# The last 512 tokens of x modulated with tokens on partitions and turned by transposing DMAs

## The chip, the cores and the metric

The kernel runs on one core of one Trainium2 chip. The metric is the device time of one execution in microseconds (us). Executions of the same kernel agree to some tenths of a per cent.

## What is computed

One decoder layer on 2048 tokens of width 1024, in float32. Cut to what matters here:

```python
mod = silu(c) @ w_ada + b_ada
shift, scale, gate = split(mod, 3)
h = rms_norm(x, g_pre) * (1.0 + scale) + shift      # modulated input
proj = h @ w_in                                     # qa ka va fa za qb kb vb zb
oa = forgetting_attention(qa, ka, va, fa + b_fgate) * silu(za)      # causal, 8 heads
ob = sliding_window_sink_attention(rope(qb), rope(kb), vb, sinks) * silu(zb)   # window 128
y = concat(oa, ob) @ w_out
x = x + gate * rms_norm(y, g_post)
```

`h` is what the change is about: each token's row is scaled by the reciprocal root of its mean square, then multiplied by a vector over the 1024 features (`g_pre * (1 + scale)`) and added to another (`shift`). The projections need `h` with the features on the partitions, in two float16 parts (high and low) whose sum carries the float32 value.

## The kernel before

Tokens are handled in four chunks of 512 (`CH`). The projection input of chunk `ci` is the tile `hT[ci]`, 128 partitions (a feature within a group of 128) by two parts by eight feature groups by 512 tokens. `hT[3]` also holds x of chunk 1 for a while, before it is filled.

How a chunk is brought there, in four helpers (chunks 1 to 3): `load_x` (L404) fetches x by SyncE, 128 tokens on the partitions. `squares` (L412) has ScalarE square and sum each tile of 128 tokens, `root` (L419) computes the reciprocal roots `rst`, three small operations on VectorE and the rest on GpSimd. `normal` (L423) multiplies each tile by its `rst` on VectorE. `turn(ci, k)` (L431) then takes feature group `k`: TensorE transposes four 128 by 128 blocks into a PSUM tile `px`; ScalarE applies the scale `Gp` and the shift `Shp` as one value for each partition, once into the float32 tile `hf` and, for even `k`, once more into the high part; VectorE makes the high part for odd `k` and subtracts it from `hf` to give the low part. `turn_x` (L450) queues the second and third step one and two ticks later. The `hf` tiles rotate among three buffers.

The order of the work is written out by hand. `punits` is a list of units of TensorE work: a kb or a z projection of a chunk is eight units of three matmuls (`proj_units`, L342), a vb projection eight units of twelve narrow ones, a turn is a unit of its own. `fill` (L1119) runs the units in order. Before unit number `n` it runs what `at_slice(n, ...)` (L1000) has put there, and every two units `tick` (L205) runs what `after(m, ...)` has deferred by `m` ticks. Every engine works through its instructions in the order in which they were issued. The weights of each projection are fetched, scaled and split by functions that `add` (L962) puts at fixed distances ahead of the first use: `w_load`, `w_max` (the maximum on VectorE and a store of 128 values `mx_d` by GpSimd), `w_back` (read back to all partitions as `mxr`), `w_scale`, `w_high`, `w_low`, `w_done`.

Three PSUM banks `bk` serve the projections in turn; a bank is taken with a group's first unit and freed by the step that empties it on VectorE: the cos step of kb (L754), the low part of vb (L807 and L809), the product of z (L392). A kb projection's rotary step swaps halves by four DMAs on SyncE's queue (`qs`, L751), needs them seven ticks later (L764), and then stores the result in `kst` by four more (L779). `spread` (L455) issues eight DMAs that fill the cosine and sine tables of a chunk.

Chunk 2 has, in this order, kb (units 64 to 71), vb, zb0 of chunk 2 and zb1 of chunks 0 and 1. Before the change the eight turns of chunk 3 stand among vb, zb0 and zb1. Then come kb and vb of chunk 3, the rest of the sliding-window attention, the forgetting attention over eight heads, and the output projection, in which the attention's result is fetched by transposing DMAs from HBM (`dma_start_transpose`, L1483).

Of the kernel before, what the change touches and what calls it, by code (L numbers as in the profile page):

```python
# [10 lines left out]
F32 = mybir.dt.float32  # L11
F16 = mybir.dt.float16
# [3 lines left out]
AF = mybir.ActivationFunctionType  # L16
ALU = mybir.AluOpType
AX = mybir.AxisListType

P = 128  # L20
S = 2048
D = 1024
KT = D // P
# [8 lines left out]
VB = P + 8  # L32
# [11 lines left out]
def hybrid_layer(  # L44
# [17 lines left out]
    V, A, G, PE, SP = nc.vector, nc.scalar, nc.gpsimd, nc.tensor, nc.sync  # L62
# [6 lines left out]
    dram = ctx.enter_context(tc.tile_pool(name="dram", bufs=1, space=DRAM))  # L69
# [7 lines left out]

    o_d = [dram.tile([CH, D], F32, name="o_d0")] + [dram.tile([4, 2, P, D], F16, name=f"o_d{t}") for t in range(1, NCH)]
    z_d = dram.tile([KT, P, S], F32, name="z_d")
    mx_d = [dram.tile([P, 1], F32, name=f"mx_d{n}") for n in range(3)]  # L80


    def sm(n, tag):
        return small.tile([P, n], F32, tag=tag, name=tag)
# [7 lines left out]
    def rsqrt_mean(dst, ss, n, eng=None):  # L92

        for _ in rsqrt_parts(dst, ss, n, eng=eng):
            pass
# [45 lines left out]
    def early_pool(name, bufs):  # L141
        return early.enter_context(tc.tile_pool(name=name, bufs=bufs, side="right", reuse_waits="tile"))

    xin, hst, vbw = early_pool("xin", 4), early_pool("hst", 3), early_pool("vbw", 1)
    trig = early_pool("trig", 1)
    swx = ExitStack()
    swc = swx.enter_context(tc.tile_pool(name="swc", bufs=1))

    hT = [(hpool if i < 2 else hlate).tile([P, 2, KT, CH], F16, name=f"hT{i}") for i in range(NCH)]
# [3 lines left out]
    Gp = const.tile([P, KT], F32, name="Gp")  # L153
    Shp = const.tile([P, KT], F32, name="Shp")
# [47 lines left out]
    def after(n, f):  # L202
        late.append([n, f])
# [198 lines left out]
    xt, rstd, xlate = {}, {}, {}  # L402
# [9 lines left out]
    def squares(ci, us=range(4)):  # L412
        if ci not in rstd:
            rstd[ci] = sm(4, "ss"), sm(4, "rst")
        for u in us:
            junk = hst.tile([P, D], BF16, tag="junk", name="junk", bufs=1)
            A.activation(junk[:], xt[ci * 4 + u], AF.Square, accum_out=rstd[ci][0][:, u:u + 1])

    def root(ci):  # L419
        ss, rst = rstd[ci]  # L420
        rsqrt_mean(rst, ss[:], 4, G if ci else None)

    def normal(ci, us=range(4)):  # L423
        for u in us:
            t, r = ci * 4 + u, rstd[ci][1][:, u:u + 1]
            if ci == 0:
                A.activation(xt[t], xt[t], AF.Copy, scale=r)
            else:
                V.tensor_scalar(xt[t], xt[t], r, None, op0=ALU.mult)

    def turn(ci, k, px=None):  # L431

        px = px or ps_x.tile([P, CH], F32, tag="x", name="px")
        for u in range(4):
            PE.transpose(px[:, u * P:(u + 1) * P], xt[ci * 4 + u][:, k * P:(k + 1) * P], ident[:])
        hf = hst.tile([P, CH], F32, tag="hf", name="hf")
        hi, lo = hT[ci][:, 0, k, :], hT[ci][:, 1, k, :]

        def scaled():
            for dst in ([hi] if k % 2 == 0 else []) + [hf[:]]:  # L440
                A.activation(dst, px[:], AF.Identity, scale=Gp[:, k:k + 1], bias=Shp[:, k:k + 1])

        def split():
            if k % 2:
                V.tensor_copy(hi, hf[:])
            V.tensor_tensor(lo, hf[:], hi, op=ALU.subtract)

        return scaled, split

    def turn_x(ci, k):  # L450
        scaled, split = turn(ci, k)
        after(1, scaled)
        after(2, split)

    def spread(g):  # L455

        gr, gc = slice(32 * g, 32 * g + 32), slice(g * CH, (g + 1) * CH)
        for r in range(4):
            rr = slice(32 * r, 32 * r + 32)
            SP.dma_start(cosT[rr, gc], cs_[gr, :])  # L460
            SP.dma_start(sinT[rr, gc], (sp_ if r % 2 else sn_)[gr, :])
# [4 lines left out]
    with tc.manual_schedule():  # L466
# [94 lines left out]
        rest, parts = TWO_PI, []  # L561
# [211 lines left out]
    def kb_units(ci):  # L773
        cols_ = slice(ci * CH, (ci + 1) * CH)

        def finish(stg):
            for g in range(2):
                for h in range(2):
                    SP.dma_start(kst[g][64 * h:64 * h + 64, :, cols_], stg[64 * g:64 * g + 64, :, :])  # L779

        return proj_units("kb", ci, evac_rope(ci, finish, stp))
# [178 lines left out]
    pkeys, punits = [], []  # L960

    def add(key, us):  # L962
        if key in ("va01", "va23"):
            for j in key[2:]:
                add(f"va{j}", [])
        elif key not in pkeys and key not in ("kb", "vb"):
            at = len(punits) - {"za3": 4}.get(key, 20 if key[:2] == "za" else 0)
            for n, (lead, f) in enumerate(((42, lambda: w_load(key, pieces(key))), (31, lambda: w_max(key)),
                                           (21, lambda: w_back(key)), (12, lambda: w_scale(key)),
                                           (9, lambda: w_high(key)), (7, lambda: w_low(key, 0)),  # L970
                                           (5, lambda: w_low(key, 1)), (4, lambda: w_done(key)))):
                if n >= 4 and key[:2] in ("qk", "za"):
                    lead -= 1
                if n < 4 and key == "qb0":
                    lead += (16, 14, 12, 4)[n]
                if key[:2] in ("zb", "va"):
                    lead += {"va0": 26, "va2": 26, "zb3": 18}.get(key, 8)
                if n == 0 and key in ("qk1", "za0"):
                    lead += 8
                if key == "zb1":  # L980
                    lead = at - (6, 38, 46, 67, 71, 73, 75, 77)[n]
                if key == "zb0":
                    if n >= 3:
                        events.setdefault((13, 13, 14, 15, 16)[n - 3], []).append(f)
                else:
                    events.setdefault(max(at - lead, n), []).append(f)
        if key not in pkeys:
            pkeys.append(key)
        punits.extend(us)
# [10 lines left out]
    def at_slice(n, f):  # L1000
        events.setdefault(n, []).append(f)
# [17 lines left out]
    for ci in range(NCH):  # L1019
        n0 = len(punits)  # L1020
        add("kb", kb_units(ci))
        add("vb", vb_units(ci))
        if ci < 3:
            add(*others[ci])
            if ci == 2:
                add(*others[4])
                add(*others[5])

            mine, punits[n0:] = punits[n0:], []
            at_ = ([14, 16, 17, 18, 19, 20, 21, 22], [6, 8, 10, 12, 14, 16, 18, 20], [14, 16, 18, 20, 22, 24, 26, 28])[ci]  # L1030
            for n, u in enumerate(mine):
                punits.append(u)
                if n in at_:
                    punits.append(lambda ci=ci, k=at_.index(n): turn_x(ci + 1, k))
            if ci < 2:

                for u in range(4):
                    at_slice(n0 + (24 if ci else 9) + u, lambda ci=ci, u=u: squares(ci + 2, (u,)))
                    at_slice(len(punits) + (4 if ci else -10) + u, lambda ci=ci, u=u: normal(ci + 2, (u,)))
                at_slice(len(punits) - (3 if ci else 18), lambda ci=ci: root(ci + 2))  # L1040
            at_slice((12, 22, 30)[ci], lambda ci=ci: spread(ci + 1))
    n0 = len(punits)
    at_slice(n0, lambda: open_fox())
# [287 lines left out]
    class Step:  # L1331
# [30 lines left out]
        def low(self):  # L1362
            V.tensor_tensor(self.ph[:, 1, :self.w], self.p32[:, :self.w], self.ph[:, 0, :self.w], op=ALU.subtract)  # L1363
# [271 lines left out]
    with tc.manual_schedule():  # L1635
# [35 lines left out]
        for s, stp_ in enumerate(steps):  # L1671
            hd, r = divmod(s, NS)
# [111 lines left out]
```

## Time and profile before

| | |
|---|---|
| median of 3 runs | 1157.41 us (1156.38 to 1158.7) |
| the profiled execution | 1157.8 us |
| its span, first to last instruction | 1156.1 us |
| TensorE busy | 1116.8 us, 97% |
| VectorE busy | 930.5 us, 80% |
| ScalarE busy | 661.4 us, 57% |
| kb of chunk 2, first matmul | 90.9 us |
| kb of chunk 3, first matmul | 123.63 us |

How to read it: a line of the timeline has the start and the length in us, the engine (PE TensorE, PEld its weight load, DVE VectorE, ACT ScalarE, POOL GpSimd, SPq the queue of SyncE), the line of the program, the operation, output and inputs by the program's names, the count, and in brackets the idle time before it with what ended it. A line of the groups has the count, the busy time in us and the mean length of one in ns. A line of the waits has who waited for whom, us in total, how often, and the longest. A line of the windows has the stretch, then for each engine the busy time and count, then the granted TensorE clock, the DMA share and GB/s.

### The profile page before, as it was taken

The numbers are of one execution on the slowest core, as the hardware profiler recorded it, in microseconds if no ns is written. First come the engines' busy times: TensorE is split into PE (matmuls) and PEld (weight loads), VectorE is DVE, ScalarE is ACT, GpSimd is POOL, SyncE is SP. The second block draws the span as 40 slices with busy tenths as digits, with TensorE's granted clock in tenths as the row PEclk, the third lists the DMA queues.
The fourth block names the chain that finished last, engine by engine and source line by source line (L and its number), as shares of the span: only waits on it lengthen the run. The fifth ranks groups of instructions, "written<-read, shape, count | busy, mean of one in ns | idle before, by whom it ended". The sixth has DMA issues, their size and how long they took to land. (4 is left out here: it accounts for less than half of the span.)

```text
span 1156.1 us, 25291 instructions
## 1 busy us (share of the span) xinstructions
PE 1116.8 (97%) x9869; PEld 656.3 (57%) x9869; DVE 930.5 (80%) x2137; ACT 661.4 (57%) x1150; POOL 207.5 (18%) x332
## 2 busy tenths in 40 slices
PE   5899999999999999999999999999999999999997
PEld 2475544577765866555555555555555555544444
DVE  7877468987888568788988899888888887878885
ACT  2876344654555421666757666666776778534332
POOL 1122134554556530010010110001000000000000
PEclk9899999999999999999999999999999999999999
DMA  9943355433243232442344342123311337686743
GB/s 333 336 116 72 87 78 96 97 63 90 52 92 88 58 87 58 73 108 29 80 64 87 84 67 70 38 49 76 45 43 34 91 101 206 140 225 197 199 135 109
DMA packets 123476, 120.10 MB, mean 104 GB/s; under 512 B 64948, under 2 KB 100828, under 8 KB 123356
## 3 DMA queue, kind: packets, MB, share of 16 engines
q1 hardware_dynamic: 112088, 85.69, 27.6%
q0 software_dynamic: 10832, 32.50, 13.5%
q8 instruction: 77, 1.26, 0.6%
q14 instruction: 43, 0.35, 0.1%
q10 hardware_dynamic: 436, 0.28, 0.1%
HBM read 64.75 MB, written 25.18 MB: 78 GB/s over the span
## 5 line engine op out<-in xcount | busy, mean ns | idle before, releaser
L1356 ACT ACTIVATE p<-sta,lift,scl_qk 128x1024 f32<-128x1024 f32 (+2 forms) x160 | 172.0, 1075 | 131.6 <-PE sta L1350 82.6
L351 PE MATMUL bk<-hT,wh_qk 128*128 128x512 f16 x768 | 194.7, 378 | 0.0
L1363 DVE TENSOR_TENSOR pha<-p,pha 128x1024 f16<-128x1024 f32 (+2 forms) x160 | 169.1, 1057 | 0.2 <-ACT pha L1360 0.2
L1303 DVE TENSOR_REDUCE a_m<-bk 128x1 f32<-128x512 f32 x192 | 130.4, 686 | 45.8 <-PE bk L1300 44.8
L1576 PE MATMUL bk<-wohl,oz 128*128 128x512 f16 x744 | 165.3, 379 | 1.1 <-DVE oz L1525 0.7
L1360 ACT ACTIVATE pha<-p 128x1024 f16<-128x1024 f32 (+2 forms) x160 | 148.1, 926 | 5.9 <-PE poa L1376 1.2
L1576 PEld LDWEIGHTS <-oz 128*128 128x128 f16 x744 | 71.9, 99 | 82.8 <-DVE oz L1525 1.8
L1376 PE MATMUL poa<-vt,pha 128*128 128x65 f16 x1088 | 116.1, 192 | 1.4 <-DVE pha L1363 1.2
L1373 PE MATMUL poa<-vt,pha 128*128 128x65 f16 x1088 | 116.6, 193 | 0.8 <-DVE ona L1382 0.7
L1375 PE MATMUL poa<-vt,pha 128*128 128x64 f16 x1088 | 116.6, 194 | 0.0
L351 PEld LDWEIGHTS <-wh_qk 128*128 128x128 f16 x768 | 72.1, 97 | 74.4 <-issue 2.1
L1349 PE MATMUL sta<-T 128*128 128x512 f16 (+1 forms) x320 | 110.9, 346 | 2.8 <-ACT p L1356 2.7
L1300 PE MATMUL bk<-T 66*128 66x512 f16 (+2 forms) x320 | 109.7, 348 | 2.4 <-DVE a_m L1303 1.9
L1373 PEld LDWEIGHTS <-pha 128*128 128x128 f16 x1088 | 101.5, 96 | 15.5 <-DVE ona L1382 1.9
L1350 PE MATMUL sta<-T 69*128 69x512 f16 (+1 forms) x320 | 109.8, 348 | 0.0
L1375 PEld LDWEIGHTS <-pha 128*128 128x128 f16 x1088 | 100.9, 97 | 11.4
L1376 PEld LDWEIGHTS <-pha 128*128 128x128 f16 x1088 | 100.8, 99 | 1.8 <-DVE pha L1363 1.7
L351 PE MATMUL bk<-hT,wh_za 128*128 128x512 f16 x384 | 99.7, 378 | 0.0
L369 PE MATMUL bk<-wh_va,hT 128*128 128x256 f16 x768 | 91.9, 273 | 0.0
L351 PE MATMUL bk<-hT,wh_zb 128*128 128x512 f16 x384 | 91.6, 379 | 0.2 <-DVE qc L754 0.2
L351 PE MATMUL bk<-hT,wh_qb 128*128 128x512 f16 x384 | 91.2, 379 | 0.0
L369 PEld LDWEIGHTS <-hT 128*128 128x128 f16 x768 | 73.3, 98 | 12.2 <-issue 2.1
(459 smaller groups left out, 1919.7 us busy)
## 6 DMA issues: line engine op xcount, KB each, us to landing
hT<-in_x_dram SPq DMA_DIRECT2D x20, 512.0 KB
wa<-in_w_ada_dram SPq DMA_DIRECT2D x16, 512.0 KB
z_d<-tz POOLq DMA_DIRECT2D x32, 256.0 KB, 3.0
T<-z_d SPq DMA_DIRECT2D x16, 512.0 KB
T<-stq SPq DMA_DIRECT2D x62, 128.0 KB
out_dram<-hT SPq DMA_DIRECT2D x15, 512.0 KB
xt<-in_x_dram SPq DMA_DIRECT2D x12, 512.0 KB
qs<-qf SPq DMA_DIRECT2D x80, 64.0 KB
```

What stands on the lines that cost most here:

```text
L351: PE.matmul(ps, whl[:, a, k, :], hT[ci][:, b, k, :], start=(k == 0 and n == 0), stop=(k == KT - 1 and n == 2))
L369: PE.matmul(ps[:, (u % 2) * 2 * P:(u % 2 + 1) * 2 * P], hT[ci][:, a, k, u * P:(u + 1) * P], wv[p][:, b, k, :], start=(k == 0 and n == 0), ...
L1303: V.tensor_reduce(m3[:, u, pc:pc + 1], mx[:, :w], axis=AX.X, op=ALU.max)
L1349: PE.matmul(self.st[:, o:o + w], T[:, 3, kb_], T[:, 1, qc], start=True, stop=False)
L1350: PE.matmul(self.st[:, o:o + w], T[0:XR, 2, kb_], T[0:XR, 0, qc], start=False, stop=not diag)
L1356: A.activation(self.p32[:, :self.w], self.st[:, :self.w], AF.Exp, scale=scl[f"qk{self.hd}"][:], bias=lift[:])
L1360: A.activation(self.ph[:, 0, :self.w], self.p32[:, :self.w], AF.Copy)
L1363: V.tensor_tensor(self.ph[:, 1, :self.w], self.p32[:, :self.w], self.ph[:, 0, :self.w], op=ALU.subtract)
L1373: PE.matmul(po[:, u, :], ph[:, 0, pq], vt[:, b, hd, 0:65], start=(self.first and n == 0 and u == 0), stop=False)
L1375: PE.matmul(po[:, u, 0:64], ph[:, 0, pq], vt[:, b, hd, 65:VW], start=False, stop=False)
L1376: PE.matmul(po[:, u, :], ph[:, 1, pq], vt[:, b, hd, 0:65], start=False, stop=(self.last and n == len(self.blocks) - 1))
L1576: PE.matmul(py, self.hl[:, i, k, :], w_slot(8 * j + k)[:, cc], start=(k == 0 and m_ == 0), stop=(k == KT - 1 and m_ == 2))
```

## The change

For chunk 3 alone the turns go. The scale and shift vectors, which lie as columns (`Gp`, `Shp`, 128 by 8), are stored to HBM as two rows of 1024 (`store_cols`) and read back to all partitions as `rowG` and as a row in the buffer of vb's raw weights (`fetch_rows`). `flat(3, u)` takes a tile of 128 tokens as it lies: two VectorE operations over 1024 features (times `rst` times the scale row, plus the shift row), a ScalarE copy to float16 one tick later (high part), a VectorE subtraction another tick later (low part), and two transposing DMAs on SyncE's queue, out of the two parts into `hT[3]`. The parts use the rotating `hf` buffers. The eight turns leave the list, so all later units come eight positions sooner, with their deferred work and the weight functions counted from them. The squares of chunk 3 move from units 56 to 59 to units 46, 48, 50 and 52, its root from 61 to 55; the normal steps at 68 to 71 are replaced by `flat` at 64, 70, 76 and 82. Chunks 0 to 2 keep their way.

```diff
+    g_d = dram.tile([2, D], F32, name="g_d")
...
-    trig = early_pool("trig", 1)
+    trig, rowp = early_pool("trig", 1), early_pool("rowp", 1)
+    rowG = rowp.tile([P, D], F32, name="rowG")
...
+    rows_ = []
+
+    def store_cols():
+        for n, col_ in enumerate((Gp, Shp)):
+            SP.dma_start(g_d[n].rearrange("(k p) -> p k", p=P), col_[:])
+
+    def fetch_rows():
+        rows_.append(vbw.tile([P, KT, VB], F32, tag="wraw", name="rowS")[:].rearrange("p k n -> p (k n)")[:, 0:D])
+        for n, row_ in enumerate((rowG[:], rows_[0])):
+            SP.dma_start(row_, g_d[n].partition_broadcast(P))
+
+    def flat(ci, u):
+
+        t, r = ci * 4 + u, rstd[ci][1][:, u:u + 1]
+        parts = [hst.tile([P, D], F16, tag="hf", name="hh") for _ in range(2)]
+        V.scalar_tensor_tensor(xt[t], xt[t], r, rowG[:], op0=ALU.mult, op1=ALU.mult)
+        V.tensor_tensor(xt[t], xt[t], rows_[0], op=ALU.add)
+
+        def low():
+            V.tensor_tensor(parts[1][:], xt[t], parts[0][:], op=ALU.subtract)
+            for b in range(2):
+                SP.dma_start_transpose(hT[ci][:, b, :, u * P:(u + 1) * P], parts[b][:])
+
+        after(1, lambda: A.activation(parts[0][:], xt[t], AF.Copy))
+        after(2, low)
...
-            at_ = ([14, 16, 17, 18, 19, 20, 21, 22], [6, 8, 10, 12, 14, 16, 18, 20], [14, 16, 18, 20, 22, 24, 26, 28])[ci]
+            at_ = ([14, 16, 17, 18, 19, 20, 21, 22], [6, 8, 10, 12, 14, 16, 18, 20], [])[ci]
...
-            if ci < 2:
-
+            if ci == 0:
                 for u in range(4):
-                    at_slice(n0 + (24 if ci else 9) + u, lambda ci=ci, u=u: squares(ci + 2, (u,)))
-                    at_slice(len(punits) + (4 if ci else -10) + u, lambda ci=ci, u=u: normal(ci + 2, (u,)))
-                at_slice(len(punits) - (3 if ci else 18), lambda ci=ci: root(ci + 2))
+                    at_slice(9 + u, lambda u=u: squares(2, (u,)))
+                    at_slice(22 + u, lambda u=u: normal(2, (u,)))
+                at_slice(14, lambda: root(2))
+            if ci == 1:
+                at_slice(20, store_cols)
+                at_slice(34, fetch_rows)
+                for u in range(4):
+                    at_slice(46 + 2 * u, lambda u=u: squares(3, (u,)))
+                    at_slice(64 + 6 * u, lambda u=u: flat(3, u))
+                at_slice(55, lambda: root(3))
```

## The prediction

> **What bounds the kernel now.** I read the page first (busy time, slices), then the stretch of the change by windows, then its timeline engine by engine, then the waits and SyncE's queue.
>
> ```profile
> span 1156.1 us, 25291 instructions
> ...
> PE 1116.8 (97%) x9869; PEld 656.3 (57%) x9869; DVE 930.5 (80%) x2137; ACT 661.4 (57%) x1150; POOL 207.5 (18%) x332
> ...
> PE   5899999999999999999999999999999999999997
> ```
>
> TensorE (PE) is busy from the second slice to the last, so whatever shifts its work near 100 us shifts the end by as much: all later work is issued by position in the list of PE units, not by time. The change acts between the kb projection of chunk 2 (units 64 on) and that of chunk 3. Units are the entries of the list `punits`; chunk 2 has 40 of them beside its eight turns.
>
> ```profile
> 90.90 4.70 PE L351 MATMUL bk<-hT,wh_kb 128*128 128x512 f16 x21
> 97.02 0.38 PE L351 MATMUL bk<-hT,wh_kb 128*128 128x512 f16 x1 [1.43 <-DVE hT L445]
> ...
> 105.04 0.81 PE L351 MATMUL bk<-hT,wh_zb 128*128 128x512 f16 x3 [0.22 <-DVE qc L754]
> ...
> 107.42 0.60 PE L435 MATMUL px<-ident,xt 128*128 128x128 f32 x4
> ...
> 109.15 0.60 PE L435 MATMUL px<-ident,xt 128*128 128x128 f32 x4
> ...
> 123.63 5.34 PE L351 MATMUL bk<-hT,wh_kb 128*128 128x512 f16 x24
> ...
> 128.81 5.84 PE L795 MATMUL bk<-wh_vb,hT 128*128 128x136 f16 x96
> ...
> 134.49 1.67 PE L351 MATMUL bk<-hT,wh_qb 128*128 128x512 f16 x7
> ```
>
> A group of 24 matmuls takes 128.81 - 123.63 = 5.18 us, a vb group 134.49 - 128.81 = 5.68. Chunk 2 is one kb, one vb and three z groups: 4 x 5.18 + 5.68 = 26.4 us of 123.63 - 90.90 = 32.7. Two z units and one turn take 109.15 - 107.42 = 1.73; two z units alone 2 x 5.18 / 8 = 1.30; so a turn costs PE 0.43, not the 4 x 0.27 of its records, and eight cost 3.5 us. The remaining 2.8 are waits, most of them the one of 1.43 for `hT` of chunk 2 and its neighbours. So PE could save 6.3 us at most.
>
> ```profile
> 90.00:123.60 33.60, 31.46 (x229) 19.18 (x228) 22.85 (x49) 19.68 (x34) 7.23 (x19) 1.00 0.34 77
> ```
>
> In the same stretch VectorE (DVE) works 22.85 of 33.6 us. It has room before, but the change adds to it and shortens the stretch.
>
> **Part by part: the sizes.** The new operations have near relatives of the same shape.
>
> ```profile
> L1363 DVE TENSOR_TENSOR pha<-p,pha 128x1024 f16<-128x1024 f32 x96 | 116.8, 1217 | 0.2 <-ACT pha L1360 0.2
> ...
> L1360 ACT ACTIVATE pha<-p 128x1024 f16<-128x1024 f32 x96 | 101.2, 1054 | 2.1
> ...
> L441 ACT ACTIVATE hf<-px,Shp,Gp 128x512 f32<-128x512 f32 x30 | 22.9, 781 | 2.8 <-DVE hT L446 2.3 <-PE px L435 0.4
> ...
> L446 DVE TENSOR_TENSOR hT<-hf,hT 128x512 f16<-128x512 f32 x32 | 22.0, 692 | 5.5 <-ACT hf L441 5.0
> ...
> L1605 DVE SCALAR_TENSOR_TENSOR hT<-hT,y_rs 128x1024 f32<-128x1024 f32 x15 | 19.2, 1277 | 0.0
> ...
> L1506 DVE TENSOR_TENSOR T<-of,T 128x1024 f32<-128x1024 f32 x12 | 14.7, 1225 | 0.5
> ...
> L445 DVE CAST hT<-hf 128x512 f16<-128x512 f32 x16 | 6.8, 426 | 0.3 <-ACT hf L441 0.2
> ...
> L429 DVE TENSOR_SCALAR xt<-xt,rst 128x1024 f32<-128x1024 f32 x8 | 5.9, 787 | 2.4 <-POOL rst L122 2.4
> ```
>
> DVE loses 4 x 0.79 (normal) + 4 x 0.43 (casts) + 8 x 0.69 (low parts) = 10.4 us and gains 4 x (1.28 + 1.23 + 1.22) = 14.9 (scale by row, add row, low part). ScalarE (ACT) loses 12 x 0.78 = 9.4 and gains 4 x 1.05 = 4.2. PE loses the 3.5. DVE then has 22.9 + 4.5 = 27.4 us of work in a stretch that PE wants to do in 26.4: DVE is the bound of the stretch, and the order of its queue decides.
>
> **When the new work can start.** `flat(0)` needs `rst` of chunk 3. Before, that waited for the squares, which ACT did among the last turns of chunk 2 (this also caused PE's wait of 1.43). They now come earlier, so this wait goes. But `root(3)` stands behind the rotary step of kb(1), L764, in DVE's queue.
>
> ```profile
> 78.53 2.44 SPq L751 DMA_DIRECT2D qs<-qf  x4
> ...
> 78.78 0.54 POOL L230 DMA_DIRECT2D mx_d<-w_mx  x1 [0.50 <-DVE w_mx L227]
> ...
> 87.32 0.69 DVE L764 TENSOR_TENSOR qs<-qs,sinT 128x512 f32<-128x512 f32 x1 [3.32 <-DMA qs<-qf]
> ...
> 95.87 0.17 DVE L101 TENSOR_SCALAR rs_v<-ss 128x4 f32<-128x4 f32 x1 [1.52 <-ACT junk L417]
> ...
> 96.34 0.22 POOL L108 TENSOR_SCALAR rs_v<-rs_v 128x4 f32<-128x4 f32 x1 [9.02 <-DVE rs_h L106]
> ...
> 100.44 0.20 POOL L122 TENSOR_TENSOR rst<-rs_t,rs_y 128x4 f32<-128x4 f32 x1
> ```
>
> L764 and L765 end at 87.32 + 1.4 = 88.7, one low part and the root's three small operations at 89.9, and GpSimd's (POOL's) part takes 100.64 - 96.34 = 4.3: `rst` at 94.3, by when DVE has done the last parts of chunk 2.
>
> **DVE's queue from 94.3.** In program order, with what the helpers queue by position:
>
> ```profile
> 98.21 0.28 DVE L246 TENSOR_REDUCE w_mx<-mxr 128x1 f32<-128x128 f32 x1
> ...
> 99.10 0.15 DVE L253 TENSOR_SCALAR w_sw<-w_sw 128x1 f32<-128x1 f32 x1
> ...
> 103.65 0.74 DVE L273 SCALAR_TENSOR_TENSOR wh_zb<-wr_zb,w_sw,wh_zb 128x512 f16<-128x512 f32 x1
> ...
> 104.31 0.68 DVE L754 SCALAR_TENSOR_TENSOR qc<-bk,cosT 128x512 f32<-128x512 f32 x1
> ...
> 107.49 1.22 DVE L227 TENSOR_REDUCE w_mx<-wr_qb 128x1 f32<-128x1024 f32 x1 [0.38 <-DMA wr_qb<-in_w_in_dram]
> ```
>
> flat(0) 2.5 to 96.8; a z evacuation 0.7; `w_scale` of zb1 (98.21 to 99.25) 1.0; low(0) 1.2 to 99.7; flat(1) 2.5 to 102.2; half of zb1's low weights 0.7; low(1), which waits for ACT's copy of 1.05, to 104.5; the cos step of kb(2) 0.7 to 105.2. That step frees the bank that zb0(2) needs: PE, there at 90.9 + 5.18 + 5.68 = 101.8, waits 3.4 us and starts zb0(2) at 105.2, where it starts before. So the 2.2 us that kb(2) won are lost again here, and only the turns behind remain. Next, the other half of zb1's weights and `w_max` of qb0 (which the shorter list moves before flat(2)) end at 107.0, flat(2) at 109.5, zb1's last and vb's evacuation at 110.5.
>
> **The transposing DMAs.** SyncE (SP) issues two for each tile, behind low(u); they also free the three `hf` buffers: low(2) on DVE writes the buffer that the first transpose of flat(1) reads, low(1) that of flat(0).
>
> ```profile
> L1483 SPq DMA_TRANSPOSE T<-o_d x24: 1244/1480/3466, 981.3 to 1098.6; - x24
> ```
>
> ```profile
> 100.94 2.48 SPq L751 DMA_DIRECT2D qs<-qf  x4
> ...
> 108.62 0.68 DVE L764 TENSOR_TENSOR qs<-qs,sinT 128x512 f32<-128x512 f32 x1
> ```
>
> ```profile
> 1067.00:1068.00 1.00, 1.00 (x7) 0.42 (x5) 0.16 (x1) 1.00 (x1) 0.00 (x0) 1.00 0.91 221
> ```
>
> They read HBM there, SBUF here; issue takes 1.24 to 3.47 us, I take 1.45. The landing of one is not shown. At least 256 KB at 221 GB/s, 1.2 us; at most 108.62 - 103.42 = 5.2 (four swaps beside a 512 KB load that nobody waited for). I take 2.2, near the lower end, since little else moves at 120 us. On SP: pair 0 from 99.8 to 102.7 (low(1) waits little); kb(2)'s swap, released by ACT, 103.7 to 106.2; pair 1 from 106.2, its first landing at 109.9 when nothing disturbs it.
>
> **What disturbs it.** The swap issued at 78.53 to 80.97 was held until 87.3. No data moved any more (the last two columns are the DMA share and GB/s):
>
> ```profile
> 83.00:83.50 0.50, 0.50 (x11) 0.50 (x8) 0.47 (x2) 0.00 (x0) 0.00 (x0) 1.00 0.00 0
> ```
>
> ```profile
> POOL mxr L235 <- DMA mx_d<-w_mx: 15.5, 2, 8.1
> ```
>
> What was open was `mx_d`, 128 writes of 4 bytes issued at 78.78; GpSimd's wait for it, here twice, lasts to about 8.1 us from its issue, and the swap behind it landed half a microsecond later. The swap of kb(2), with no `mx_d` open, was ready before 108.62. So a small store holds back the completion of what is queued behind it. Now `w_max` of qb0 ends at 107.0, its `mx_d` goes out at 107.05, and pair 1 (data from about 108) falls into it: landing at 115.3, not 109.9. Low(2) waits from 110.6 to 115.4; vb's second evacuation, flat(3), L764 and L765 and low(3) follow: 115.4 + 1.2 + 0.6 + 2.5 + 1.4 + 1.2 = 122.3; pair 3: 2.9 + 2.2, `hT3` complete at 127.4. The first kb unit of chunk 3 needs both parts of all tokens: 127.4 against 123.63, 3.8 later. Its first matmul of three needs the high part alone, 0.2 less, and the same working done on the rows of before puts kb(3) 0.2 late, 0.2 less: **+3.4 us**. The Trainium skill, "DMA: Bandwidth & Descriptors", section "Queues, rings and completion order", says that a DMA's semaphore increment lands only after every earlier write of that DMA engine, across its queues. By that rule the transposing DMAs are held as the swap was (+3.4); without it the sum is -1.4; the trace agrees for the plain swap, no row here shows it for a transposing DMA.
>
> **Store and rows.** `store_cols` and `fetch_rows` add four issues of some 0.5 us on SP, ahead of kb(1)'s swap (to 80.5 to 83.0), which is held to 87.3 anyhow: nothing, as long as the fetch finds the store landed. Between them SP issues two `spread` and a `kst`:
>
> ```profile
> 65.24 0.57 SPq L460 DMA_DIRECT2D cosT<-cs__234  x1
> ...
> 77.85 0.59 SPq L461 DMA_DIRECT2D sinT<-sp__232  x1
> ```
>
> That is 65.2 to 78.4, a cover of 13 us, here some 66 to 79.5.
>
> The profiled execution took 1157.8 us for a span of 1156.1, 0.4 above the median of 1157.41; on the median, 1157.4 + 3.4 = **1160.8 us**.
>
> **The rivals.** (1) *Transposes are not held.* Low(2) starts at 110.7, `hT3` is complete at 122.6, kb(3) starts 1.1 to 1.4 earlier than before: 1156.0. For it: it decides whether pair 1's first landing comes before `mx_d`'s writes begin, and the margin is some 2 us (109.9 against 108). (2) *PE stays the bound*: DVE's operations start earlier than I think or the bank wait at zb0 vanishes; up to 6.3 us less, 1151.1. Against it: 27.4 us of DVE work for 26.4. (3) *The fetch waits for the column store*: two stores of 1024 writes of 4 bytes, 16 times `mx_d`. If such writes are served one by one at some 6 us for 128 (8.1 less about 2 of a plain landing, an estimate), 16 x 6 = 96 us, less 13 of cover: 83 late on SP, and the swap, DVE and PE behind: 1240. Served eight at a time it is 12 us and costs nothing; it decides from 13 us on. Each 512-byte stretch gets 128 of the writes, as `mx_d`'s did, and there are 16 stretches, so I hold overlap for likelier. The Trainium skill, same page, "Rules for kernel authors", says that a last dimension that isn't contiguous lowers to one descriptor per element; this speaks against the change, and no row here shows such a store. (4) *Transposes out of SBUF take longer*: issue 2.5 instead of 1.45 adds 2 x 1.05 at the end and 1 to 1.5 at low(1): 1164.4; with the row's 3.47 about 1168.
>
> **How the numbers follow.** Chances: forecast (1159 to 1163.5) 0.43, (1) 0.22, (2) 0.15, (3) 0.10, (4) 0.10. A measurement of this kernel can tell about 0.2%, 2.3 us, from no change. Faster by more: (2) and a third of (1), 0.22. Within: the rest of (1) and the low edge of the forecast, 0.20. Slower: 0.58. The range leaves out most of (2) and of (3): 1154 to 1168.5. The cases on the slow side alone span 1159 to 1168.5.
>
> **What would show it.** Right: PE's wait at kb(2)'s end gone; a PE wait of about 3 us for L754 at the first zb0 unit; a DVE wait of 4 to 5 us at the third low part, on a transposing DMA while `mx_d` is open; PE waiting for `hT3` by DMA at the first kb unit, some 127 us. Wrong: no DVE wait on a DMA there (rival 1); kb(3) near 117 (2); SP standing at the fetch (3); transposes above 2 us on SP (4).

## The result, and the profile after

| | before | after |
|---|---|---|
| median | 1157.17 us (1156.38 to 1158.7, 4 runs) | 1173.11 us (1170.17 to 1174.61, 4 runs) |
| the profiled execution, its span | 1157.8, 1156.1 | 1174.61, 1172.9 |

The ratio after to before is 1.0134, 95% interval 1.0122 to 1.0147: 15.9 us slower, where 3.4 were predicted and 1168.5 was the end of the range. The side was right; the size was not.

The page of the changed kernel first:

```profile
span 1172.9 us, 25226 instructions
...
PE 1120.8 (96%) x9837; PEld 653.7 (56%) x9837; DVE 934.0 (80%) x2133; ACT 656.3 (56%) x1142; POOL 209.3 (18%) x332
...
PE   5895999999999998999999999999999999999997
PEclk9898999999999999999999999999999999999999
```

TensorE is busy 4 us longer, though it has 32 fewer matmuls, and its granted clock has a dent in the fourth slice (88 to 117 us). TensorE's timeline from kb(2) to qb0 (the lines that were L351, L795, L754 are now L353, L823, L782; L446 and L445 are L448 and L447):

```profile
91.20 2.97 PE L353 MATMUL bk<-hT,wh_kb 128*128 128x512 f16 x13
100.45 1.01 PE L353 MATMUL bk<-hT,wh_kb 128*128 128x512 f16 x2 [6.28 <-DVE hT L448]
102.42 3.96 PE L353 MATMUL bk<-hT,wh_kb 128*128 128x512 f16 x9 [0.95 <-DVE hT L447]
106.22 3.00 PE L823 MATMUL bk<-wh_vb,hT 128*128 128x136 f16 x48
109.49 3.00 PE L823 MATMUL bk<-wh_vb,hT 128*128 128x136 f16 x48 [0.27 <-DVE tz L394]
117.05 18.61 PE L353 MATMUL bk<-hT,wh_zb 128*128 128x512 f16 x72 [4.55 <-DVE qc L782]
136.29 0.38 PE L353 MATMUL bk<-hT,wh_kb 128*128 128x512 f16 x1 [0.63 <-DVE w_mx L248]
137.46 2.75 PE L353 MATMUL bk<-hT,wh_kb 128*128 128x512 f16 x12 [0.80 <-DMA hT<-hh]
```

qb0 follows at 148.10, 13.6 us later than before (134.49). The brackets add up to 13.5 us of waits. From kb(2) to qb0 the kernel before took 43.6 us: 37.3 of groups, 3.5 of turns, 2.8 of waits. This one takes 56.9: the same 37.3, no turns, 13.5 of waits, and 6.1 us more. Those 6.1 are in the lengths: nine matmuls in 3.96 us, where 24 took 5.34. The windows show why (after the stretch: PE, PEld, DVE, ACT, POOL, the granted clock, the DMA share, GB/s):

```profile
94.20:99.40 5.20, 0.00 (x0) 0.00 (x0) 0.99 (x2) 0.00 (x0) 0.00 (x0) 0.97 0.40 119
99.40:105.90 6.50, 4.35 (x10) 1.37 (x10) 5.22 (x14) 3.88 (x6) 4.30 (x12) 0.50 0.33 77
105.90:112.50 6.60, 6.32 (x98) 5.85 (x97) 6.03 (x10) 2.21 (x2) 1.81 (x4) 1.00 0.58 151
112.50:116.40 3.90, 0.00 (x0) 0.00 (x0) 3.35 (x5) 1.88 (x4) 0.00 (x0) 0.97 0.50 93
116.40:123.00 6.60, 5.95 (x15) 2.04 (x15) 5.64 (x10) 1.39 (x3) 0.54 (x1) 0.50 0.61 119
```

The clock falls inside the first and the fourth row, some 0.3 us before their ends (hence 0.97): 4.9 us after the last matmul the first time, 3.7 us the second. Each time TensorE then has half its clock for 6.8 us.

The first wait is for a low part that stands behind the sine step of kb(1) (now L792) in VectorE's queue. That step waits for the swap, and the swap stands in SyncE's queue behind the store and the fetch:

```profile
66.87 0.50 SPq L461 DMA_DIRECT2D g_d<-Gp  x1
67.48 0.55 SPq L461 DMA_DIRECT2D g_d<-Shp  x1
...
71.56 0.59 SPq L489 DMA_DIRECT2D sinT<-sn__238  x1
78.26 0.51 SPq L488 DMA_DIRECT2D cosT<-cs__239  x1
...
84.27 0.59 SPq L489 DMA_DIRECT2D sinT<-sp__237  x1
87.56 0.51 SPq L488 DMA_DIRECT2D cosT<-cs__239  x1
...
90.01 0.58 SPq L466 DMA_DIRECT2D rowG<-g_d  x1
90.70 0.40 SPq L466 DMA_DIRECT2D rowS<-g_d  x1
91.19 2.70 SPq L779 DMA_DIRECT2D qs<-qf  x4
```

SyncE issues nothing from 72.2 to 78.3 and from 84.9 to 87.6. Its waits name the store for the first of the two, and a `kst` store for the second:

```profile
SPq L488 <- DMA g_d<-Gp: 6.1, 1, 6.1
...
SPq L488 <- DMA kst<-stb: 2.7, 1, 2.7
```

`L488` fetches a cosine table and reads neither of them. The trace shows why it waits all the same: the program's DMAs on this queue take turns on eight semaphores (100 and 102 to 108), and a DMA is issued only when the one that used its semaphore before, eight DMAs earlier, is complete. All 37 waits in the sixteen traces (over 0.3 us, from 55 to 1100 us) in which SyncE stood until a DMA landed are for the DMA eight issues back. The store, issued at 66.87, was complete at 78.2, 11.4 us later. `kst` came late by that, at 79.52, and so fell in with zb1's small store (`mx_d`, issued at 79.08, read back from 87.62); it was complete at 87.5.

The swap goes out 12.7 us later than before (78.53), and VectorE follows:

```profile
98.38 0.69 DVE L792 TENSOR_TENSOR qs<-qs,sinT 128x512 f32<-128x512 f32 x1 [12.19 <-DMA qs<-qf]
...
106.30 1.28 DVE L472 SCALAR_TENSOR_TENSOR xt<-xt,rst,rowG 128x1024 f32<-128x1024 f32 x1 [1.54 <-POOL rst L123]
...
127.58 1.23 DVE L476 TENSOR_TENSOR hh<-xt,hh 128x1024 f16<-128x1024 f32 x1 [5.47 <-DMA hT<-hh]
```

The sine step is 11.1 us later than before (87.32), `flat(0)` 12.0 later than predicted. The third line is the predicted hold of the third low part: 5.47 us, 4.8 were predicted.

From 148 on the kernel gains 2.0 us (a wait of 1.9 at 201 in the sliding-window attention is gone) and loses 5.2 near 440, at two projections of the forgetting attention. There SyncE brings four transfers for the same tile, and GpSimd issues a small store (`mx_d`) beside them. SyncE's and GpSimd's timelines before:

```profile
426.46 0.60 SPq L1077 DMA_DIRECT2D T<-stq  x1
427.11 0.60 SPq L1078 DMA_DIRECT2D T<-stq  x1
...
427.18 0.56 POOL L230 DMA_DIRECT2D mx_d<-w_mx  x1 [7.54 <-DVE w_mx L227]
```

and after, with TensorE's:

```profile
438.11 1.35 SPq L1111 DMA_DIRECT2D T<-stq  x1
439.50 0.60 SPq L1112 DMA_DIRECT2D T<-stq  x1
...
438.83 0.56 POOL L232 DMA_DIRECT2D mx_d<-w_mx  x1 [7.54 <-DVE w_mx L229]
...
446.51 0.23 PE L1334 MATMUL bk<-T 66*128 66x128 f16 x1 [3.85 <-DMA T<-stq]
```

The third issue takes 1.35 us instead of 0.60, so the fourth goes out behind the small store instead of ahead of it and TensorE waits 3.85 us for the tile. The rest of the 5.2 us is half clock again, from 447 to 450.5. In all: 0.3 (kb(2) starts at 91.20 instead of 90.90) + 13.3 - 2.0 + 5.2 = 16.8, the difference of the spans.

### The profile page after: what moved, and what is told of

Same layout as the page of the kernel before. It is cut to its first block, busy times and chain, and to the rows that moved or that the text cites. A ratio compares the mean times of both kernels' runs of the same rounds, so it can differ in the third digit from the quotient of the medians.

```text
span 1172.9 us, 25226 instructions
## 1 busy us (share of the span) xinstructions
PE 1120.8 (96%) x9837; PEld 653.7 (56%) x9837; DVE 934.0 (80%) x2133; ACT 656.3 (56%) x1142; POOL 209.3 (18%) x332
## 5 line engine op out<-in xcount | busy, mean ns | idle before, releaser
L353 PE MATMUL bk<-hT,wh_qk 128*128 128x512 f16 x768 | 196.3, 380 | 0.0
L353 PEld LDWEIGHTS <-wh_qk 128*128 128x128 f16 x768 | 72.5, 98 | 75.2 <-issue 3.5
L1409 PEld LDWEIGHTS <-pha 128*128 128x128 f16 x1088 | 100.9, 97 | 11.4
L353 PE MATMUL bk<-hT,wh_za 128*128 128x512 f16 x384 | 99.7, 378 | 0.0
L353 PE MATMUL bk<-hT,wh_zb 128*128 128x512 f16 x384 | 93.4, 388 | 4.6 <-DVE qc L782 4.6
L353 PE MATMUL bk<-hT,wh_qb 128*128 128x512 f16 x384 | 91.2, 379 | 0.0
```

Of the source, the lines that this page charges most:

```text
L353: PE.matmul(ps, whl[:, a, k, :], hT[ci][:, b, k, :], start=(k == 0 and n == 0), stop=(k == KT - 1 and n == 2))
L1409: PE.matmul(po[:, u, 0:64], ph[:, 0, pq], vt[:, b, hd, 65:VW], start=False, stop=False)
```

## The experiments

Each kernel's profiled execution is read at the same marks. The last column is the time from the small store near 430 us to the end of the span; it shows the late wait.

| kernel | median us (before beside it) | kb(1)'s swap, sine step | kb(2), kb(3), qb0 | store near 430 to end |
|---|---|---|---|---|
| before | 1157.17 | 78.53, 87.32 | 90.90, 123.63, 134.49 | 728.9 |
| after | 1173.11 (1157.17) | 91.19, 98.38 | 91.20, 136.29, 148.10 | 734.1 |
| e2 store alone | 1162.19 (1157.84) | 88.25, 92.56 | 90.77, 129.57, 140.43 | 728.2 |
| e8 fetch alone | 1163.25 (1157.78) | 80.06, 92.15 | 90.85, 128.88, 139.74 | 728.5 |
| e1 wide store | 1172.96 (1157.84) | 81.18, 94.04 | 91.69, 131.96, 143.84 | 732.3 |
| e3 keep busy | 1169.72 (1157.84) | 89.47, 97.59 | 90.86, 132.21, 143.62 | 729.5 |
| e4 maximum late | 1173.23 (1157.84) | 80.42, 92.47 | 90.68, 128.92, 141.75 | 734.0 |
| e5 fetch later | 1176.10 (1157.78) | 80.25, 92.56 | 90.72, 131.41, 144.70 | 737.6 |
| e6 maximum early | 1175.29 (1157.78) | 80.69, 94.27 | 90.84, 132.57, 143.43 | 737.5 |
| e7 four parts | 1169.36 (1157.78) | 80.52, 94.29 | 90.94, 128.48, 139.34 | 736.0 |
| e9 pad | 1171.98 (1157.60) | 93.25, 99.56 | 91.13, 138.59, 152.08 | 729.6 |
| e10 rows early | 1171.63 (1157.60) | 83.83, 92.02 | 91.15, 130.88, 142.85 | 735.8 |
| e11 all | 1162.63 (1157.60) | 80.61, 90.11 | 91.27, 127.02, 137.88 | 729.1 |
| e12 order | 1157.39 (1158.22) | 81.64, 94.56 | 92.29, 124.08, 134.94 | 728.8 |
| e13 order, no pad | 1162.88 (1158.22) | 84.08, 95.37 | 92.90, 124.89, 135.75 | 728.6 |
| e14 root behind | 1154.93 (1157.87) | 81.92, 91.87 | 92.22, 121.39, 132.25 | 729.3 |

The kernels with `flat` scatter by 3 to 9 us from run to run, the kernel before by 2 to 4; single profiles are therefore read at the marks, not by their span alone.

**e2, the store alone.**

```diff
 (before.py)
+    def store_cols():
...
+            if ci == 1:
+                at_slice(20, store_cols)
```

> The kernel before with the two column stores alone, which nothing reads. Theory S: SyncE's queue stands some 6 and 3 us, kb(1)'s swap goes out near 90, VectorE's sine step comes near 98, TensorE waits some 6 us in kb(2) and has half the clock for some 5 us after it: 1157.2 + 6.3 - 1.4 (the wait that was there) + 2.7 = 1165. Rival (SyncE stands for the fetch, not for the store): 1157 to 1158.

Measured: ratio 1.0039 (1.0024 to 1.0054), 4.4 us. SyncE's waits name the store here too, with no fetch in the kernel:

```profile
SPq L465 <- DMA g_d<-Gp: 5.9, 1, 5.9
```

The mechanism is as expected (the swap at 88.25, then half clock from 99.2 to 106.0), the size smaller: VectorE's sine step moved by 5.2 us and not by 11, since the swap then went out after zb1's small store had landed (read back from 87.73) and was done 4.3 us later.

**e8, the fetch alone** (with a store that transposes the columns first and writes sixteen pieces of 512 bytes).

```diff
 (before.py)
+        for n, col_ in enumerate((Gp, Shp)):
+            PE.transpose(px[0:KT, n * P:(n + 1) * P], col_[:], ident[:])
...
+            SP.dma_start(g_d[:].rearrange("n (k p) -> k n p", p=P), turned_.rearrange("k (n p) -> k n p", n=2))
...
+        after(1, lambda: A.activation(turned_, px[0:KT, 0:2 * P], AF.Copy))
+        after(2, out_)
...
+                at_slice(20, store_cols)
+                at_slice(34, fetch_rows)
```

> The kernel before with the wide store and the fetch of the two rows ahead of kb(1)'s swap, which nothing reads. Theory Q (what stands ahead of the swap in SyncE's queue delays it, the 1 MB of the fetch as well as the 4-byte store): the sine step of kb(1) comes near 94 as in e1 instead of 87.3, TensorE waits in pieces in kb(2), the clock drops to half there; 1160 to 1162, as the column store alone gave. Rival (the fetch is harmless by itself and e1's loss comes from the new VectorE work): the sine step at 88, 1157 to 1158.

Measured: ratio 1.0047 (1.0034 to 1.006), 5.5 us; the sine step at 92.15. So the fetch (with the small wide store, which has no run of its own) costs as much as the 4-byte store. At the sine step the two add up: 4.8 and 5.2 us late by themselves, 11.1 in the changed kernel. That their times add up to 9.9 of the 15.9 us isn't shown: in the changed kernel the waits behind the sine step overlap with others, and taking one cause away does not give its share back (see e1 and e10).

**e1, the wide store in the changed kernel.**

> Theory S (the store of the columns in 4-byte pieces fills SyncE's queue and delays what stands behind it): with the two rows stored as 16 pieces of 512 bytes, SyncE has no gap of 6 us, the swap of kb(1) goes out by 83 instead of 91.2, the sine step ends by 89, TensorE's wait in kb(2) is below 2 us instead of 6.3 and the clock stays at 1.00 there; about 1161, what the prediction gave for the rest of the change. Theory F (the new VectorE work and its order cost the time, whatever the store does): TensorE still waits 4 us or more in kb(2) and for the first zb0 unit; 1169 or more.

Measured: no gain in the median, 1.0134 (1.01 to 1.0169). Theory S fell as it stood: SyncE no longer stands and the swap goes out at 81.18, yet the sine step comes at 94.04. The timelines of SyncE and VectorE, and the windows:

```profile
80.00 0.60 SPq L474 DMA_DIRECT2D rowG<-g_d  x1
80.70 0.39 SPq L474 DMA_DIRECT2D rowS<-g_d  x1
81.18 3.36 SPq L787 DMA_DIRECT2D qs<-qf  x4
...
94.04 0.69 DVE L800 TENSOR_TENSOR qs<-qs,sinT 128x512 f32<-128x512 f32 x1 [7.36 <-DMA qs<-qf]
...
79.00:83.00 4.00, 4.00 (x64) 3.98 (x63) 3.04 (x6) 2.94 (x5) 0.61 (x2) 1.00 1.33 222
83.00:90.00 7.00, 7.00 (x66) 5.20 (x64) 1.90 (x6) 6.24 (x15) 0.54 (x1) 1.00 0.15 32
90.00:93.50 3.50, 3.50 (x18) 1.61 (x17) 0.00 (x0) 0.00 (x0) 0.00 (x0) 1.00 0.72 214
```

Before the change the swap's data had moved when zb1's small store (issued at 78.78) stopped everything until 87. Now 1 MB of rows stands ahead of it: part of it moves at 222 GB/s, then 7 us of next to nothing, and the rest and the swap come at 90 to 93.5. In its profile kb(3) is 4.3 us earlier than in the changed kernel, but the median of the four runs, which lie 9 us apart, isn't.

**e5, the fetch six units later.** `at_slice(40, fetch_rows)` instead of 34.

> The changed kernel with the wide store (e1) and the fetch six units later, behind kb(1)'s swap. Theory Q: the swap goes out at 78 to 80, the sine step comes at 87 to 88.5 as before the change, rst near 94, TensorE waits less than 1.5 us in kb(2) and keeps its clock there; the waits for the first zb0 unit (3 to 5 us) and the hold of the third low part (5 us) stay; 1160 to 1164. Rival (VectorE's order decides whatever the queue does): as e1, 1169 to 1173.

Measured: 1.0154 (1.0141 to 1.0167). It tells nothing on theory Q: the swap is issued later in the program than I had thought, and the fetch (79.09) still stood ahead of it (80.25).

**e10, rows early.** Store at unit 8, fetch at unit 21.

> The changed kernel with the wide store at unit 8 instead of 20 and the fetch at unit 21 instead of 34, ahead of the eight issues of the tables, so that its 1 MB has moved when kb(1)'s swap goes out. Theory Q: the swap goes out near 80, the sine step comes at 87 to 88.5, TensorE waits less than 1.5 us in all in kb(2) and keeps its clock there; kb(3) comes some 4 to 6 us earlier than in e1 (131.9): 126 to 128; 1165 to 1168 with the wait at 446 still there. Rival (VectorE's order): as e1, kb(3) near 132, 1170 to 1173.

Measured: 1.0116 (1.0098 to 1.0134), nearer to the rival. The fetch went out at 66.2, but SyncE then stood for 2.5 us (72.1 to 74.6), so the swap went out at 83.83, in the middle of the small store's time; the sine step came at 92.02. TensorE's waits in kb(2) were pieces of at most 1.4 us and its clock held until 109. Then the wait for the first zb0 unit (4.56) and the hold of the third low part (6.40) came as in the changed kernel.

**e3, matmuls in the waits.**

```diff
+                at_slice(68, lambda: warm(24))
+                at_slice(80, lambda: warm(16))
```

> The changed kernel, with 24 matmuls whose result nobody reads before the fifth kb(2) unit and 16 before the first zb0 unit of chunk 2, where TensorE waited 6.3 and 4.6 us. Theory C (the half clock comes from TensorE's idle time): the matmuls lie in the waits, the clock stays at 1.00 from 90 to 125, and the 2.7 and 3.0 us that the half clock cost are gone: 1173.1 - 5.7 = 1167.4. Rival (the half clock has another cause): the clock still falls to 0.50 near 99 and 116, 1173 or more.

Measured: 1.0101 (1.0084 to 1.0119), 3.4 us below the changed kernel. The second stretch of half clock is gone, the first lasts 3.4 us instead of 6.8 (theory C had expected none):

```profile
99.50:105.00 5.50, 3.82 (x10) 1.24 (x10) 4.33 (x13) 3.43 (x6) 4.19 (x12) 0.69 0.37 88
105.00:125.00 20.00, 18.10 (x154) 11.19 (x152) 18.00 (x29) 5.47 (x9) 2.46 (x5) 1.00 0.70 124
```

kb(3) starts at 132.21 instead of 136.29. The half clock comes from TensorE's idle time, and adds more than half to the 10.8 us of the two waits that bring it about (6.1 in the changed kernel). Most of these 4 us are lost again in waits before 430; the end gains 4.6 us because the late wait is gone too, which was not expected (see e9).

**e4, the maximum of qb0's weights behind the last transposing DMA.**

```diff
-                    lead += (16, 14, 12, 4)[n]
+                    lead += (16, -1, 0, -2)[n]
```

> The wide store of e1, and the maximum of qb0's weights (with its 128 writes of 4 bytes) moved from unit 75 to unit 90, behind the last transposing DMAs. Theory H (those writes hold the transposing DMAs): the third low part waits less than 1 us, the first kb(3) unit does not wait for the transposed tile, 3 to 4 us less than e1: about 1157. Rival (the transposing DMAs land late by themselves): the third low part waits about 5 us as in the changed kernel, and the time is that of e1.

Measured: 1.0132 (1.0094 to 1.0169), as e1. VectorE's timeline:

```profile
115.64 1.23 DVE L484 TENSOR_TENSOR hh<-xt,hh 128x1024 f16<-128x1024 f32 x1 [0.56 <-ACT vb L839]
...
138.03 0.29 DVE L248 TENSOR_REDUCE w_mx<-mxr 128x1 f32<-128x128 f32 x1 [7.50 <-DMA mxr<-mx_d]
```

Theory H holds: the third low part waits 0.56 us instead of 5.45, and TensorE runs into kb(3) without a wait, where it waited 0.98 and 0.86 us in e1. So the hold cost TensorE 1.8 us there. (kb(3)'s second matmul comes 4.3 us earlier than e1's, 3.3 when kb(2)'s start is taken off; the rest lies ahead of kb(3) and isn't the hold alone, since e1 has two stretches of half clock there and e4 one.) But now the read-back is late: VectorE stands 7.50 us for it, and the gain is given back at qb0 and later.

**e6 and e7, the maximum early; four buffers.** `lead += (36, 33, 33, 4)[n]`; e7 also has `early_pool("hst", 4)`.

> As e5, and the maximum of qb0's weights with its 128 writes of 4 bytes moved ahead of the transposing DMAs (unit 75 to 56, load and read-back with it) instead of behind them as in e4. Theory H (those writes hold the transposing DMAs): the third low part waits less than 1 us, no TensorE wait for the transposed tile, nor for qb0's weights as in e4; 3 to 5 us less than e5: 1156 to 1160. Rival: the transposes land late by themselves, as e5.

> As e6 with four buffers instead of three for the parts and the turns. If the buffers are what VectorE waits for in flat, the low parts wait nowhere on a transposing DMA and the chain is up to 1.5 us shorter than e6; if VectorE's own work is the bound, it is as e6 within 1 us.

Measured: e6 1.0149 (1.0136 to 1.0162), e7 1.0097 (1.0078 to 1.0117). In e6 the reduction stood behind the late sine step, so the store went out at 102.4 instead of ahead of the transposes and held the second low part (3.06 us) instead of the third. With a fourth buffer no low part waits for a transpose, the wait for zb0 falls from 5.4 to 2.7 us, and the half clock behind it (3.4 us in e6) is gone: 5.9 us, more than the 1.5 expected. Both kept the fetch ahead of the swap.

**e9, 32 tiny transposes** at 26 us, whose result nobody reads.

```diff
+        for _ in range(32):
+            PE.transpose(bk[0][0:2, 2 * P:3 * P], ident[:, 0:2], ident[:])
```

> The changed kernel with 32 tiny transposes whose result nobody reads, at 26 us where TensorE waits 4 us for a weight: as many TensorE instructions as the turns had taken out of the program. Theory K (TensorE's program, now 32 instructions shorter ahead of 430 us, is fetched in 16 KB pieces some 10 us later against the work; the piece that comes at 438 lengthens SyncE's issue to 1.35 us, which puts the next transfer behind a small store, and TensorE waits 3.8 us at 446 and runs at half clock after it): that wait is gone, SyncE's issue is 0.60, all else is as it was; 1173 - 5.5 = 1167.5. Rival (the wait at 446 follows from the time at which the stage ends): it stays, 1173.

Measured: 1.0125 (1.0111 to 1.0138), no gain in the median; its profile lost 2.3 us more before kb(3) and 1.7 more up to qb0, and gained 4.5 at the end (729.6). Ahead of qb0 its swap went out 2.1 us later, and the first stretch of half clock lasted 10.2 us instead of 6.8; why the swap came later is open. The late wait itself fell from 3.8 to 1.1 us, and the SyncE issue was 0.60. The page counts the program's pieces of 16 KB among the DMA queues:

```profile
q8 instruction: 77, 1.26, 0.5%
```

The records of this queue have a time for each. That it is TensorE's is inferred, from their moving with TensorE's instructions. Against the small store near 430 us:

| kernels | program piece | SyncE's third issue | late wait |
|---|---|---|---|
| before, e2, e8, e3, e9, e11, e12, e14 | 9.8 to 10.2 us ahead | 0.60 | 0 to 1.1 |
| after, e1, e4, e5, e6, e7, e10 | 0.9 to 1.2 ahead | 1.16 to 1.47 | 3.6 to 4.1 |
| e13 | 1.0 ahead | 0.99 | 0 |

The first row has the turns, or at least as many other TensorE instructions put in; the others have 32 transposes fewer. What the change took out of TensorE's program moved the fetch of a piece by 9 us against the work, on to SyncE's issue. That such a fetch makes the issue longer is argued from their meeting: in the sixteen traces, from 60 us on, 188 of the 693 plain issues of SyncE that overlap with a piece of this queue take more than 0.9 us, and 68 of the 6157 others. So it is far likelier there, but three in four that meet a piece stay below that. The Trainium skill, "Runtime: NRT & Kernel Launch", section "Instruction fetch mechanics", says that an engine's program is refilled in blocks of 16 KiB by DMA and that crossing a block is mostly hidden. That is said of the engine whose program it is; here the fetch went with a longer issue on another engine.

**e11, all of these:** wide store at 8, fetch at 21, four buffers, the maximum at unit 50, the 32 tiny transposes.

> e10 with the 32 tiny transposes of e9, four buffers for the parts, and the maximum of qb0's weights at unit 50, ahead of the sine step in VectorE's queue and of the root in GpSimd's, so that its 4-byte writes are over before the first transposing DMA. If rows, small store and program fetch together are the cause, what is left is VectorE's own work: the wait for the first zb0 unit of 2 to 4 us against 3.5 us of turns saved, kb(3) between 121 and 125; 1155 to 1160. If VectorE's work is the larger cost, kb(3) after 127 and 1162 or more.

Measured: 1.0046 (1.0029 to 1.0062), 1162.63: the slow side of the two. Sine step at 90.11, no hold, no late wait. What is left is the wait for the first zb0 unit, 4.56 us, with half clock behind it.

**e12 and e13, VectorE's order.** On e11:

```diff
-                    at_slice(46 + 2 * u, lambda u=u: squares(3, (u,)))
-                    at_slice(64 + 6 * u, lambda u=u: flat(3, u))
-                at_slice(55, lambda: root(3))
+                    at_slice(24 + 2 * u, lambda u=u: squares(3, (u,)))
+                    at_slice((52, 65, 75, 80)[u], lambda u=u: flat(3, u))
+                    at_slice((60, 72, 76, 81)[u], lambda u=u: flat_out(3, u))
+                at_slice(36, lambda: root(3))
```

`flat` keeps the two operations over the rows, `flat_out` has the rest. e13 is e12 without the 32 transposes.

> e11 with the new VectorE work put where VectorE stood idle: squares at units 24 to 30, root at 36, the two operations over the rows at 52 (before the sine step, where VectorE waits 3.3 us), 65, 75 and 80, the copy, low part and transposing DMAs of each tile at 60, 72, 76 and 81, so that the cos step of kb(2) has one tile's work ahead of it and not two. Theory O (what is left in e11 is the order of VectorE's queue: 4.6 us of wait for the first zb0 unit, 2.9 us of half clock behind it, 1.3 us of wait in vb): those go, kb(3) comes at 119 to 121 instead of 127.0 (123.6 before the change), and the end is 2 to 5 us before the kernel before: 1153 to 1156. Rival (VectorE's sum of work bounds the stretch, wherever it is put): kb(3) after 124, 1159 or more.

> e12 without the 32 tiny transposes. Theory K (where a 16 KB piece of TensorE's program is fetched decides the wait near 440 us): SyncE's third issue of T is again 1.2 to 1.4 us long there, TensorE waits 3.5 to 4 us, 4 to 6 us more than e12. Rival (that wait came from the times at which the stage ended in the earlier kernels): as e12 within 1 us.

Measured: e12 1.0000 (0.9991 to 1.0009), e13 1.0035 (1.0019 to 1.005). In e12 the wait for zb0 is 0.3 us and the clock stays at 1.00 from 55 us to the end's last slices; all of the 15.9 us are back, but kb(3) is at 124.08 and not at 119 to 121: the root's work on GpSimd now stood ahead of the load of qb0's weights, and VectorE waited 5.5 us for them. e13 is 5.5 us above e12, the size that theory K gives, but its mechanism isn't shown here: the eight runs lie at 1159 to 1160 or at 1162 to 1166, and the profiled one (1159.24) had the longer issue but not the wait. Its span is 2.5 us above that of e12, and all of it came ahead of 430. That the runs at 1162 to 1166 have the late wait is likely, but none was profiled, and why the others escape wasn't tried.

**e14, the root at unit 40.**

> e12 with the root at unit 40 instead of 36. In e12 the root's 5 us on GpSimd stood ahead of the issue of qb0's weights and of zb1's small store, so that VectorE waited 5.5 us for those weights and kb(1)'s sine step came at 94.6 instead of 90.1 as in e11. If that is all, GpSimd issues the load at 78 and the small store at 80, the sine step comes at 89 to 91, TensorE waits less than 2 us in kb(2) instead of 4.1 and more, kb(3) comes at 119.5 to 121 (123.6 before the change): 1153 to 1155, faster than the kernel before. If VectorE's sum of work bounds the stretch, kb(3) stays near 124 and the time at 1157.

Measured: 0.9976 (0.9966 to 0.9986), 1154.93 against 1157.87: 2.9 us faster than the kernel before. TensorE:

```profile
92.22 3.62 PE L353 MATMUL bk<-hT,wh_kb 128*128 128x512 f16 x16
96.14 1.24 PE L353 MATMUL bk<-hT,wh_kb 128*128 128x512 f16 x5 [0.31 <-DVE hT L448]
98.55 0.38 PE L353 MATMUL bk<-hT,wh_kb 128*128 128x512 f16 x1 [1.17 <-DVE hT L447]
99.28 0.59 PE L353 MATMUL bk<-hT,wh_kb 128*128 128x512 f16 x2 [0.35 <-DVE hT L448]
99.70 5.84 PE L837 MATMUL bk<-wh_vb,hT 128*128 128x136 f16 x96
105.85 15.70 PE L353 MATMUL bk<-hT,wh_zb 128*128 128x512 f16 x72 [0.31 <-DVE qc L796]
121.39 5.34 PE L353 MATMUL bk<-hT,wh_kb 128*128 128x512 f16 x24
```

From kb(2) to kb(3) it takes 29.2 us, 32.7 before. That is the 3.5 us of the turns, the part of the prediction's rival (2) that could be had; kb(2) itself starts 1.3 us later than before, the squares now stand among the turns of chunk 2.

## Why the prediction was wrong, step by step

**The step that failed is "Store and rows": four issues of half a microsecond, "nothing, as long as the fetch finds the store landed".** It asked only whether the fetch would wait for the store. The fetch did find it landed (11.4 us after the store's issue, and the fetch went out 23 us after it), and it cost all the same. Two other things decided. The store was still open when its semaphore's turn came again, eight DMAs later, so SyncE's own queue stood 6.1 us ahead of the fetch, and 2.7 more for the `kst` store that this had pushed beside zb1's small store. And the fetch's 1 MB went ahead of the swap in the same queue, so that the swap's data no longer moved before zb1's small store closed the way. In the kernel before, each alone cost 4.4 and 5.5 us, and both came out at the sine step, which the prediction had rightly named as what `root(3)` stands behind. Rival (3) had the right place, the store, but its price was 83 us or nothing, with a chance of 0.10; the truth lay between, with the swap late by 12.7 us. Its sign, SyncE standing, did show, but ahead of the fetch and not at it. The prediction had quoted the hold of that same swap and concluded that being late under it costs nothing; it did not ask what happens when the swap's data have not moved yet as the hold begins. How much of the 12.5 us beyond the forecast belongs to this step isn't shown by itself: by the marks, kb(3) comes 12.7 us late where 3.4 were forecast, qb0 13.6, and the way from there to the end adds 5.2 - 2.0.

**A term that the sum lacked: the clock.** The forecast had a TensorE wait of 3.4 us and no price for what follows it. The waits took the clock to half for 6.8 us twice, 6.1 us in the stage. The Trainium skill, "TensorE: Matmul & The Clock Gate", section "Seeing it yourself", shows the clock being lowered 5.2 us after the last matmul; here it fell 4.9 us after the matmul that ended at 94.2 and 3.7 us after the one that ended at 112.5.

**A step that was not thought of: the program itself.** That fewer TensorE instructions move the program's fetch against SyncE's issues, for 5.2 us near 440 us, was in none of the cases. e9's profile shows that as many instructions put back bring the third issue back to 0.60 us and the late wait down to 1.1; how the fetch makes an issue longer stays open.

**Right in mechanism and nearly in size:** VectorE's operations (1.28, 1.22 and 1.22 us against 1.28, 1.23, 1.22); the transposing DMAs (2.91 us for two issues against 2 x 1.45; the last landed 1.9 us after its issue, against 2.2); the wait for L782 at the first zb0 unit (4.55 against 3.4); the hold of the third low part by qb0's small store (5.47 against 4.8), shown by e4. What the hold costs TensorE was forecast too high: +3.4, where it waited 0.63 + 0.80 us at kb(3) in the changed kernel and 0.98 + 0.86 in e1, since TensorE itself came there late, at half clock. **Wrong:** that PE's wait in kb(2) would go. It grew from 1.43 to 6.28 + 0.95, because the low parts of chunk 2's turns stood behind the late sine step; `rst` came at 106 and not at 94.3 for the same reason.

**"DVE is the bound of the stretch"** was an overstatement: it was the order of VectorE's queue. With the same operations e14 runs the stretch in 29.2 us, VectorE 26.1 of them busy.

Open: why the `flat` kernels scatter more from run to run, and the 2 to 3.5 us more that e5, e6, e7 and e10 lose after 430.

## What to carry to other kernels

A DMA that "costs nothing" for its reader can cost whoever stands behind it in the same queue: list what is queued behind each new transfer, both in issues (here the eighth one behind an open DMA had to wait for its semaphore) and in bytes, and ask what that one has to be ahead of. Price a wait of TensorE of some 4 us or more at up to 3 us above its length (6.1 us for two waits here), because the clock goes with it. After a change that takes instructions out, look in the profile far from the edit as well.

## What the runs showed of the hardware that was not expected

- The first of two stores of 1024 values of 4 bytes (issues of 0.5 us) was complete 11.4 us after its issue. That SyncE's queue stood 6.1 us for it is the program's doing, with its eight semaphores in turn.
- The clock fell to 0.50 also without a full stop: in e2 TensorE worked 1.94 of the 5.4 us ahead of it, in six matmuls with waits of at most 0.9 us between them. In the changed kernel it came back 5.5 and 5.9 us after TensorE had begun again. Every stretch of half clock in the sixteen traces, the one at the end aside, lasted 3.4, 6.8 or 10.2 us.
- Near the small store at 430 us, a 16 KB piece of TensorE's program that was fetched during a SyncE issue went with an issue of 0.99 to 1.47 us instead of 0.60, in all eight kernels in which the two met there; over the whole traces 27% of such meetings went with an issue above 0.9 us, against 1% of the other issues.
